# Second feed-forward block in two phases, with the down product as seven block products summed partly by adding transfers

## The chip, the cores and the metric

The kernel runs on one core of one Trainium2 chip. The metric is device time in microseconds (us). The engines are TensorE (PE, with its weight loads PEld), VectorE (DVE), ScalarE (ACT), GpSimd (POOL) and SyncE (SP). Before the change the median of three runs is 1737.13 us (1735.81 to 1737.99).

## The reference, cut to what matters

Two layers of a backbone over 512 latent and 256 context tokens, width 1024. Each layer is a mixer and then a gated feed-forward block (FFN); the change lies mainly in the FFN of the second layer, which computes only the 512 latent tokens.

```
def _swiglu(h, w_gate, w_up, w_down):
    return (jax.nn.silu(h @ w_gate) * (h @ w_up)) @ w_down
...
        x_lat = x_lat + m_lat[5] * _rms(_swiglu(h_lat, ffn_w_gate[l], ffn_w_up[l], ffn_w_down[l]), norm_post_ffn[l])
```

The hidden width is 2816, that is 22 chunks of 128 (NFC) or 11 pairs. All data are float32.

## The kernel before, in words

Every float32 operand is split into a high part H (a cast to float32r on ACT) and a low part L (a subtraction on DVE, x - H); a product is three matmuls, H by H, H by L and L by H (`mm3`). All matmuls are issued in the helper at L348, so groups of the profile go by tile names.

**The FFN** (`ffn`, called once for each layer). `first` computes the gate and up values of the first pair of chunks directly. Then, for each further pair, `product` makes the gate values (`go`) and the up values (`uo`) of 256 hidden columns for all tokens by `seven`: a block product of two by two blocks with seven instead of eight multiplications (a Strassen-Winograd form). Each of its seven blocks is 4 chunks by 3 matmuls, 12 matmuls of n = 256 columns in layer 1 and of 384 in layer 0. `seven` uses four accumulators: A and B are the two halves of one PSUM tile of two banks, `ab`; E and D are banks of their own (`sc`). A takes blocks 11, U2 and V in turn; between them ACT copies it out (L791, L801), DVE adds B to the result (L799), E (L806) and A again (L808, L809).

`pair_operands` makes what `seven` multiplies: it loads two columns of weights, each 512 KB, into two buffers `raw` (L749), adds and subtracts their halves on DVE (L752: `ws`, `raw`) and splits the sums into H (ACT, L727) and L (DVE, L728: three of 1024 columns, `wL`, and one of 512, `dL`). There are three `raw` buffers in a ring, so a load waits until the buffer of the third load before it has had its last reader; of the first weight column of a product that is the third split.

Between the gate and the up product of a pair, `acc_part` multiplies the gated values of the pair before by two row units of the down weights (128 by 1024 each, loaded and split at L671 to L673) and adds the result to `y` in SBUF: per pair 4 token tiles, 2 units, 2 column halves and 3 matmuls, 48 matmuls of 512 columns in layer 1, and a DVE addition per tile (L820). The gated values themselves are split at L1525 and L1526. After the last pair, `ending` normalises each tile of `y`, adds the residual and stores it (`post_norm`, L652 to L659).

The order on each engine is set by a list scheduler when the program is built; each engine then works strictly in that order. PSUM has eight banks: `mm` two tiles of two banks, `sc` two, `tr` two. In the second mixer, `gate` writes two token tiles into the two halves of one `mm` tile and ACT reads each half (L1418).

Of the kernel before, what the change touches and what calls it, by code (L numbers as in the profile page):

```python
# [26 lines left out]
NFC = DFF // P  # L27
EPS = 1e-6
WU = 1024
# [104 lines left out]
class Attention:  # L134
# [7 lines left out]
    half = (slice(0, 64), slice(64, P))  # L142
# [174 lines left out]
class Net:  # L317
# [3 lines left out]
    def __init__(self, ctx, tc, I, out):  # L321
        self.tc, self.nc, self.I, self.out = tc, tc.nc, I, out
        tc.nc.scalar.preload_act_table_set("silu_and_others")
        self.side = 0
        self.whole = False
        self.pinned = False
        self.turns = []
        pool = lambda name, bufs=1, **k: ctx.enter_context(tc.tile_pool(name=name, bufs=bufs, **k))
        self.cst = pool("cst")
        self.wp = pool("wp")  # L330
        self.sm = pool("sm", 4)
        self.ps = pool("ps", space=PSUM)
        self.dr = pool("dr", space=bass.MemoryType.DRAM)

    def pool(self, name, bufs=1):
        return self.tc.tile_pool(name=name, bufs=bufs, reuse_waits="tile")

    def open_pool(self, name, side="left"):
        return self.tc.alloc_tile_pool(name=name, bufs=1, side=side, reuse_waits="tile")

    def pin(self, r):

# [4 lines left out]
    def mm(self, *a, **k):  # L347
        return self.pin(self.nc.tensor.matmul(*a, **k))  # L348
# [330 lines left out]
    def mm3(self, out, stat, mov, first, last):  # L679

        mm = self.mm
        mm(out, stat[0], mov[0], start=first, stop=False)
        mm(out, stat[0], mov[1], start=False, stop=False)
        mm(out, stat[1], mov[0], start=False, stop=last)

    def gemm_T(self, pt, W, h, groups, o=0):

# [77 lines left out]
            "U2": quarter(c, 0), "S4": quarter(c, 1), "V": quarter(d, 0),  # L765
        }

    def seven(self, W, h, X, fill, then=None):

        nc, n = self.nc, h.n  # L770
        ab = self.mm_tile("ab")
        bank = {"A": ab[:, :n], "B": ab[:, 512 : 512 + n]}
        c11, c12, c21, c22 = (X[:, i, n * k : n * k + n] for i in range(2) for k in range(2))
        for wn, hn, x in SEVEN:
            new = wn in ("11", "U1", "12", "22")
            if x not in bank:
                bank[x] = self.sc_tile(x, "ED".index(x))[:, :n]
            pt = bank[x]
            (wH, wL), (hH, hL) = W[wn], h.tiles[hn]
            for k in range(4):  # L780
                for i, (a, b) in enumerate(((wH, hH), (wH, hL), (wL, hH))):
                    self.mm(
                        pt,
                        a[:, k, :],
                        b[:, k, :],
                        start=new and k == 0 and i == 0,
                        stop=k == 3 and i == 2,
                        skip_group_check=True,
                    )
            if wn == "11":  # L790
                nc.scalar.copy(c11, pt)  # L791
            elif wn == "U1":
                copy = nc.scalar.copy(c22, pt)
                if then is not None:
                    with self.tc.issue_after(copy.ins):
                        then()
                fill()
            elif wn == "12":
                nc.vector.tensor_tensor(c11, c11, pt, op=ALU.add)  # L799
            elif wn == "U2":  # L800
                nc.scalar.copy(c12, pt)  # L801
            elif wn == "22":
                nc.scalar.mul(c21, pt, -1.0)
                fill()
            elif wn == "S4":
                nc.vector.tensor_tensor(c12, c12, pt, op=ALU.add)  # L806
            else:
                nc.vector.tensor_tensor(c21, c21, pt, op=ALU.subtract)  # L808
                nc.vector.scalar_tensor_tensor(c22, pt, -1.0, c22, op0=ALU.mult, op1=ALU.subtract)  # L809
# [501 lines left out]
    def odd_mixer(self, h, fi):  # L1311
# [4 lines left out]
        with self.pool("hg") as gp:  # L1316
# [89 lines left out]
            def gate(c0, early):  # L1406
                us = self.wide_units(4 * D + c0)
                for t0 in (0, 2):
                    pt = self.mm_tile("nat").rearrange("p (a b) -> p a b", a=2)
                    s = self.wp.tile([P, WU], F32, tag="mraw", bufs=2, name="silu").rearrange("p (a n) -> p a n", a=2)  # L1410

                    def apply(x, t0=t0, s=s):
                        o = fi[:, t0 + x.start : t0 + x.stop, c0 : c0 + 512]
                        nc.vector.tensor_tensor(o, o, s[:, x, :], op=ALU.mult)

                    for a in range(2):
                        self.wide_tile(pt[:, a, :], us, h, t0 + a)
                        nc.scalar.activation(s[:, a, :], pt[:, a, :], AF.Silu)  # L1418
# [85 lines left out]
    def ffn(self, l, xp, yp, fp, pp, rp, h, ending, extra=None):  # L1504
# [7 lines left out]
        singles = [(i,) for i in range(len(tiles))]  # L1512

        gp = rp if l else fp

        def gu(x):
            return fp.tile([P, 2, 2 * n], F32, tag=x, bufs=2 if x == "go" else 1, name=x)
# [70 lines left out]
        tp.release()  # L1588
        if gp is not rp:
            rp.release()  # L1590
        end, follow, pool = ending(y)

        last = [gated(pool, k, g, u) for k in range(2)]
# [6 lines left out]
        next(follow, None)  # L1600
        if gp is rp:
            rp.release()
        return y

    def run(self):
# [11 lines left out]
        def xat(x):  # L1617
            return lambda t: x[t * P : (t + 1) * P, :]
# [132 lines left out]
        def project(l, order, yp, w, cat, xsrc):  # L1751

            rp = self.open_pool(f"r{l}")
            forms = Forms(self, order, yp.tile([P, len(order), D], F32, tag="y", bufs=1, name=f"f{l}"), rp)
            if l:
                forms.gated = [forms.gated_tiles(rp, k) for k in range(2)]
# [53 lines left out]

        def ending(ys):
            ep = self.open_pool("e1b")
            end = ender(ep, 1, 5, lat, xat(x1), lambda t: out[0, t * P : (t + 1) * P, :], None)

            def close():
                yield
                yield
                yield
                yield
                ep.release()  # L1820

            return end, close(), ep

        self.ffn(1, ha, yp, fp, pp, rp, forms, ending)
        fp.release()
        yp.release()
        ha.release()
        pad.release()


@with_exitstack
# [46 lines left out]
```

## Time and profile before

| | before |
|---|---|
| median of 3 runs | 1737.13 us |
| the profiled execution | 1736.12 us, span 1734.3 us |
| PE busy | 1682.6 us (97%), 13512 matmuls |
| DVE busy | 1287.2 us (74%) |
| ACT busy | 865.9 us (50%) |
| POOL busy | 73.6 us (4%) |
| DMA | 187.22 MB, mean 108 GB/s |

Busy shares are averages over many stages. A matmul's own duration overlaps its neighbours', so the pace of PE is read from the distance of starts, or from a chain of waits that runs through PE (x12 in 1.44 us). Granted clock of PE: 0.997.

### The profile page before, as it was taken

To read this page: it belongs to the slowest core of one execution; us is meant where nothing else is said; L and a number is where in the kernel's file an instruction comes from. 1 tells how busy PE (TensorE), PEld (TensorE's weight loads), DVE (VectorE), ACT (ScalarE), POOL (GpSimd) and SP (SyncE) were. 2 spreads that over 40 slices of the span, in tenths; PEclk is the share of its full clock that TensorE was granted. 3 is DMA by queue.
4 is the path that set the end of the run, shared out by engine and by line. 5 is a ranking of instruction groups with operands and counts; after the bars stand their busy time and mean duration, and the time that the engine had idled before them with its cause. 6 is when DMAs were issued, how large, how long until landed. Compare 5 with 4: busy or idle time off the path is not lost. (4 is left out here: it accounts for less than half of the span.)

```text
span 1734.3 us, 32373 instructions
## 1 busy us (share of the span) xinstructions
PE 1682.6 (97%) x13512; PEld 1507.3 (87%) x13512; DVE 1287.2 (74%) x2061; ACT 865.9 (50%) x1496; POOL 73.6 (4%) x93
## 2 busy tenths in 40 slices
PE   6999998999999999999999999999999999999998
PEld 5899987888999888898997888889888899999997
DVE  4889668836969999796668328887865678878785
ACT  4745568746443323233346436665644654444442
POOL 1004110000000000000001000000000000000000
PEclk9999999999999999999999999999999999999999
DMA  9641022134334455452225222111114333233333
GB/s 320 195 142 39 2 64 89 58 134 146 112 95 146 138 185 167 131 180 62 74 85 190 78 73 62 45 55 51 51 61 145 110 108 100 87 107 105 97 106 122
DMA packets 169838, 187.22 MB, mean 108 GB/s; under 512 B 6454, under 2 KB 141148, under 8 KB 169692
## 3 DMA queue, kind: packets, MB, share of 16 engines
q1 hardware_dynamic: 167760, 181.56, 33.8%
q10 hardware_dynamic: 1932, 3.59, 0.6%
q8 instruction: 106, 1.74, 0.4%
q14 instruction: 40, 0.33, 0.1%
HBM read 175.66 MB, written 9.46 MB: 107 GB/s over the span
## 5 line engine op out<-in xcount | busy, mean ns | idle before, releaser
L348 PE MATMUL nat<-wH,x 128*128 128x256 f32 (+2 forms) x944 | 216.2, 319 | 5.1 <-ACT x L641 2.6
L673 DVE TENSOR_TENSOR wL<-raw,wH 128x1024 fp32r<-128x1024 f32 (+1 forms) x126 | 150.9, 1205 | 91.8 <-ACT wH L672 91.2
L727 ACT CAST wH<-raw 128x1024 fp32r<-128x1024 f32 x120 | 124.6, 1051 | 174.9 <-PE acc L348 61.3
L728 DVE TENSOR_TENSOR wL<-raw,wH 128x1024 fp32r<-128x1024 f32 x120 | 145.0, 1220 | 63.9 <-ACT wH L727 63.9
L348 PEld LDWEIGHTS nat<-wH,x 128*128 128x128 f32 x944 | 157.6, 190 | 21.5 <-ACT x L641 3.6
L348 PE MATMUL acc<-wH,gH 128*128 128x512 f32 x440 | 172.7, 393 | 0.0
L348 PE MATMUL acc<-wH,gL 128*128 128x512 f32 x440 | 171.7, 390 | 0.0
L348 PE MATMUL acc<-wL,gH 128*128 128x512 f32 x440 | 171.6, 390 | 0.0
L672 ACT CAST wH<-raw 128x1024 fp32r<-128x1024 f32 (+1 forms) x126 | 128.9, 1039 | 82.5 <-PE nat L348 25.2
L348 PE MATMUL nat<-wL,x 128*128 128x256 f32 (+2 forms) x472 | 148.6, 315 | 0.0
L820 DVE TENSOR_TENSOR y<-y,acc 128x1024 f32<-128x1024 f32 x135 | 114.6, 861 | 28.6 <-PE acc L348 25.9
L530 DVE SCALAR_TENSOR_TENSOR macc<-mraw,scT,macc 128x1024 f32<-128x1024 f32 x98 | 123.0, 1277 | 7.3 <-DMA mraw<-in_mod_w_dram 7.1
L348 PE MATMUL ff<-x,wH 128*128 128x512 f32 (+1 forms) x512 | 127.6, 340 | 0.0
L600 POOL TENSOR_TENSOR rs<-ms,neghalf 128x1 f32<-128x1 f32 (+2 forms) x62 | 57.5, 929 | 1586.2 <-DVE ms L598 1586.0
L348 PE MATMUL oproj<-wH,x 128*128 128x512 f32 x320 | 101.5, 395 | 0.0
L348 PEld LDWEIGHTS acc<-wH,gH 128*128 128x128 f32 x440 | 82.6, 188 | 19.9 <-DVE ws L752 1.7
L348 PEld LDWEIGHTS acc<-wH,gL 128*128 128x128 f32 x440 | 82.6, 188 | 17.3
L348 PEld LDWEIGHTS acc<-wL,gH 128*128 128x128 f32 x440 | 82.7, 188 | 16.2
L348 PEld LDWEIGHTS ff<-x,wH 128*128 128x128 f32 x512 | 87.4, 190 | 10.1
L348 PEld LDWEIGHTS nat<-wL,x 128*128 128x128 f32 x472 | 89.8, 190 | 5.1
L923 ACT COPY qkh<-arr 128x512 f32<-128x512 f32 x112 | 70.1, 642 | 36.3 <-DVE arr L928 32.2
L348 PE MATMUL ff<-x,wL 128*128 128x256 f32 (+1 forms) x256 | 86.2, 337 | 0.0
(344 smaller groups left out, 4043.0 us busy)
## 6 DMA issues: line engine op xcount, KB each, us to landing
mraw<-in_mod_w_dram SPq DMA_DIRECT2D x80, 512.0 KB, 4.0
raw<-in_ffn_w_gate_dram SPq DMA_DIRECT2D x44, 512.0 KB, 3.9
raw<-in_ffn_w_up_dram SPq DMA_DIRECT2D x44, 512.0 KB, 4.4
raw<-in_ffn_w_down_dram SPq DMA_DIRECT2D x44, 512.0 KB, 3.5
raw<-in_odd_w_in_dram SPq DMA_DIRECT2D x40, 512.0 KB, 3.8
mraw<-in_mod_w_dram SPq DMA_DIRECT2D x32, 256.0 KB, 6.0
raw<-in_even_w_in_dram SPq DMA_DIRECT2D x16, 512.0 KB, 3.8
x<-xr SPq DMA_DIRECT2D x14, 512.0 KB, 2.8
```

The lines of the kernel that those rows point to most:

```text
L348: return self.pin(self.nc.tensor.matmul(*a, **k))
L530: nc.vector.scalar_tensor_tensor(a, u, w, a, op0=ALU.mult, op1=ALU.add)
L600: nc.gpsimd.tensor_tensor(rs, ms, self.neghalf.to_broadcast([P, w]), op=ALU.pow)
L672: nc.scalar.copy(H[:, :m], raw[:, :m])
L673: nc.vector.tensor_tensor(L[:, :m], raw[:, :m], H[:, :m].bitcast(F32), op=ALU.subtract)
L727: self.nc.scalar.copy(H, f)
L728: self.nc.vector.tensor_tensor(L, f, H.bitcast(F32), op=ALU.subtract)
L820: nc.vector.tensor_tensor(y, y, pt, op=ALU.add)
L923: nc.scalar.copy(qkv[:, :, :, half, :], dst)
```

## The change

1. **Phase 1 (`ffn_whole`, layer 1 only).** The same `first` and the same ten pairs by `seven`, but no `acc_part` between them. All gated values stay in SBUF as float32 (`G`, 11 pairs by 2 by 512 tokens). In the last three pairs six 256 KB pieces of the down weights are loaded ahead into `early`.
2. **Phase 2 (`down`).** The whole down product is one block product of two by two blocks with seven multiplications: tokens in two halves, hidden chunks even and odd, output columns in two halves. Each of the seven products runs over 11 chunks and 2 token tiles with 3 matmuls of 512 columns, 66 matmuls. The products, in order, are 11, N3, S1, SN, 22, S3, 12. Products 11, SN and S3 accumulate in the banks X, N3 and 22 in O, S1 and 12 in Q.
3. **The sums of weight blocks** are made by DMAs that add to SBUF (`accum_op=ALU.add`), issued by POOL: 7 in product 11 (`tb` += block 01), 14 in S1 (`tb` += block 11, and `tc` = block 01 as a plain load), 14 in SN (`tb` += block 10, `tc` += block 11). `tb` is used by S1, SN and 22, `tc` by S3. The seven transfers of a set follow the seven groups of chunks (1, 1, 2, 2, 2, 2, 1 chunks; a chunk of one block is 256 KB).
4. **The sums of gated values** and all splits are made for each product and group anew, at most three groups ahead (`ahead(3)`; `wL`/`wH` four buffers, `aL`/`aH` three).
5. **PSUM banks.** Inside both FFNs A has two banks of its own, B the one `mm` tile, and in layer 1 the up product uses the `tr` banks for E and D. In the mixer's `gate` each token tile has an `mm` tile of its own.
6. **The end.** Two token tiles are finished after S3, two in product 12; of the last tile the square sum and the gating are done by halves, the first half ahead of time.

```
 def seven(...):
-        ab = self.mm_tile("ab")
-        bank = {"A": ab[:, :n], "B": ab[:, 512 : 512 + n]}
+        bank = {"A": self.ps.tile([P, 512], F32, tag="one", bufs=2, name="a")[:, :n]}
...
-                bank[x] = self.sc_tile(x, "ED".index(x))[:, :n]
+                bank[x] = (self.mm_tile("b") if x == "B" else self.tr_tile(x) if turned else self.sc_tile(x, "ED".index(x)))[:, :n]
...
 def mm_tile(self, name):
-        return self.ps.tile([P, 1024], F32, tag="mm", bufs=2, name=name)
+        return self.ps.tile([P, 1024], F32, tag="mm", bufs=1 if self.narrow else 2, name=name)
...
 def gate(c0, early):
-                    pt = self.mm_tile("nat").rearrange("p (a b) -> p a b", a=2)
...
+                        pt = self.mm_tile("nat")[:, :512]
+                        self.wide_tile(pt, us, h, t0 + a)
+                        nc.scalar.activation(s[:, a, :], pt, AF.Silu)
...
+    def ffn_whole(self, l, xp, yp, fp, pp, rp, h, ending):
...
+        for idx in range(1, np_):
+            c0 = 2 * idx
+            g = other if idx % 2 else go()
+            self.seven(self.pair_operands(tp, wg, c0 * P, [tp], 2), h, g, nothing, todo)
...
+            x = G[:, idx]
+            self.seven(self.pair_operands(tp, wu, c0 * P, [tp], 2), h, x, nothing, None, True)
...
+    def down(self, dp, G, early, y, tiles, n, ending):
...
+        add = lambda o, src: self.pin(nc.gpsimd.dma_start(out=o, in_=src, accum_op=ALU.add))
...
+        seven = (("11", "X"), ("N3", "O"), ("S1", "Q"), ("SN", "X"), ("22", "O"), ("S3", "X"), ("12", "Q"))
...
+            nc.scalar.copy(H, src)
+            nc.scalar.copy(a[0], f)
+            v.tensor_tensor(L, src, H.bitcast(F32), op=ALU.subtract)
+            v.tensor_tensor(a[1], f, a[0].bitcast(F32), op=ALU.subtract)
+            if name == "11":
+                v.tensor_tensor(f, A[1, 0][:, i], f, op=ALU.subtract)
+                add(t[:, i], B(0, 1, i))
+            elif name == "S1":
+                add(t[:, i], B(1, 1, i))
+                self.pin(nc.gpsimd.dma_start(out=t3[:, i], in_=B(0, 1, i)))
+            elif name == "SN":
+                add(t[:, i], B(1, 0, i))
+                add(t3[:, i], B(1, 1, i))
...
+                elif name == "S3":
+                    plus(y1[:, low], b)
+                    plus(y1[:, high], b, ALU.subtract)
+                    end(y1, tiles[nh + i])
+                    if i == nh - 1:
+                        close = final(dp, y0, tiles[i])
+                else:
+                    plus(y0[:, low], b)
+                    if i < nh - 1:
+                        end(y0, tiles[i])
+                    else:
+                        close()
```

Three places in the built order carry the prediction. The first is DVE in the steady part of the pairs of layer 1. Before, while PE runs the gate product, DVE stands like this (`go` is the product being emptied, the other rows prepare the next one), and the y additions of `acc_part` follow:

```order
L799 TENSOR_TENSOR go<-go,ab 128x256
L752 TENSOR_TENSOR ws<-raw 128x512
L752 TENSOR_TENSOR raw<-raw 128x512
L728 TENSOR_TENSOR dL<-ws,dH 128x512
L752 TENSOR_TENSOR raw<-raw 128x512
L728 TENSOR_TENSOR wL<-raw,wH 128x1024
L806 TENSOR_TENSOR go<-go,E 128x256
L752 TENSOR_TENSOR raw<-raw 128x512
L728 TENSOR_TENSOR wL<-raw,wH 128x1024
L808 TENSOR_TENSOR go<-go,ab 128x256
L809 SCALAR_TENSOR_TENSOR go<-ab,go 128x256
L728 TENSOR_TENSOR wL<-raw,wH 128x1024
```

After, one product of phase 1 on DVE is the whole of the following; `b`, `E` and `a` are the banks of the product being emptied (its output here is `early`), all other rows prepare the next product.

```order
L759 TENSOR_TENSOR ws<-raw 128x512
L805 TENSOR_TENSOR early<-early,b 128x256
L759 TENSOR_TENSOR raw<-raw 128x512
L735 TENSOR_TENSOR wL<-raw,wH 128x1024
L759 TENSOR_TENSOR raw<-raw 128x512 x2
L735 TENSOR_TENSOR wL<-raw,wH 128x1024
L812 TENSOR_TENSOR early<-early,E 128x256
L735 TENSOR_TENSOR wL<-raw,wH 128x1024
L814 TENSOR_TENSOR early<-early,a 128x256
L815 SCALAR_TENSOR_TENSOR early<-a,early 128x256
L735 TENSOR_TENSOR dL<-ws,dH 128x512
```

What moved: nothing of another product stands between the first use of a pair of loads (`ws`, which needs both) and the third split, which frees the first `raw` buffer; the y additions and the splits of gated values and row units are gone from between.

The second place is POOL in phase 2, in product SN. Before, POOL has no DMA at all; after, these stand in one row (`tb` and `tc` are the sums of weight blocks):

```order
L1707 DMA tb<-in_ffn_w_down_dram 128x512
L1707 DMA tc<-in_ffn_w_down_dram 128x512
L1707 DMA tb<-in_ffn_w_down_dram 128x2x512
L1707 DMA tc<-in_ffn_w_down_dram 128x2x512
L1707 DMA tb<-in_ffn_w_down_dram 128x2x512
```

What moved: the additions that form the blocks stand on POOL and the DMA queue, and the transfers for `tb`, needed in the next product, alternate with those for `tc`, needed one product later.

The third place is DVE where product S3 ends and product 12, the last, begins. The first two rows belong to the second group of product 12; `y` takes the banks of S3 (`x_17213` and `x_17214`); `pn`, `ms` and `xr` normalise two finished tiles; the rows with `wL<-raw` and `aL` that follow are the third group of product 12.

```order
L1736 TENSOR_TENSOR wL<-raw,wH 128x512
L1737 TENSOR_TENSOR aL<-G,aH 128x256
L1761 TENSOR_TENSOR y_17205<-y_17205,x_17213 128x512 x2
L1761 TENSOR_TENSOR y_17205<-y_17205,x_17214 128x512
L659 TENSOR_TENSOR pn<-y_17205,gv_18070 128x1024
L605 TENSOR_SCALAR ms<-sq 128x1
L1761 TENSOR_TENSOR y_17205<-y_17205,x_17214 128x512
L666 SCALAR_TENSOR_TENSOR xr_18072<-pn,rs,xr_18072 128x1024
L1736 TENSOR_TENSOR wL<-raw,wH 128x1024
L659 TENSOR_TENSOR pn<-y_17205,gv_18070 128x1024
L605 TENSOR_SCALAR ms<-sq 128x1
L1737 TENSOR_TENSOR aL<-G,aH 128x512
```

What moved: normalising of two tiles, which before followed the last down product, now stands on DVE ahead of operands that the last product needs.

More of the change, by code (lines that the diff above doesn't have):

```diff
@@ L339, in open_pool, with banks @@
         return self.tc.alloc_tile_pool(name=name, bufs=1, side=side, reuse_waits="tile")
+    def banks(self, narrow):
+        if self.ps is not None:
+            self.ps.release()
+        self.narrow = narrow
+        self.ps = self.tc.alloc_tile_pool(name={True: "psn", False: "psw", None: "pso"}[narrow], bufs=1, space=PSUM, reuse_waits="tile")
     def pin(self, r):
@@ L677, in unit_cols, with mm3 @@
         return self.unit(w[:, c0 : c0 + n].rearrange("(k p) m -> p k m", p=P), KD, n, to=to)
-    def mm3(self, out, stat, mov, first, last):
+    def mm3(self, out, stat, mov, first, last, **k):
         mm = self.mm
-        mm(out, stat[0], mov[0], start=first, stop=False)
-        mm(out, stat[0], mov[1], start=False, stop=False)
-        mm(out, stat[1], mov[0], start=False, stop=last)
+        mm(out, stat[0], mov[0], start=first, stop=False, **k)
+        mm(out, stat[0], mov[1], start=False, stop=False, **k)
+        mm(out, stat[1], mov[0], start=False, stop=last, **k)
     def gemm_T(self, pt, W, h, groups, o=0):
@@ L1514, in ffn @@
         gp = rp if l else fp
+        self.banks(True)
         def gu(x):
@@ L1590, in ffn @@
             rp.release()
+        self.banks(False)
         end, follow, pool = ending(y)
```

200 lines of the change are left out of this document (183 added, 17 removed).

## Prediction

> **What bounds the kernel now.** First the head of the page, for the bound of the whole, then the second FFN, where the change lies, by its chain of waits and by stretches.
>
> ```profile
> PE 1682.6 (97%) x13512; PEld 1507.3 (87%) x13512; DVE 1287.2 (74%) x2061; ACT 865.9 (50%) x1496; POOL 73.6 (4%) x93
> ```
>
> PE is busy for 97% of the span, so matmuls that go away pay, unless something else takes their place. The chain of waits through one period of the second FFN (one pair of chunks), with columns start, duration, what:
>
> ```profile
> 1578.31 0.69 DVE y L820
> 1579.00 2.28 DVE wL L728 x2
> 1581.30 4.90 DMA raw<-in_ffn_w_up_dram
> 1586.22 1.06 ACT wH L727
> ...
> 1590.00 0.33 DVE uo L808
> ...
> 1593.00 1.20 DVE gL L1526 x2
> 1594.20 0.34 DVE go L799
> 1594.59 1.70 PE ab L348 x12
> 1596.29 0.12 PE D L348
> 1596.41 1.44 PE E L348 x12
> 1597.85 1.44 PE ab L348 x12
> 1599.29 10.92 PE acc L348 x48
> ```
>
> A block of twelve 256-column matmuls takes 1.44 us (0.120 each), 48 of 512 columns take 10.92 (0.2275 each). PE waits once per product for DVE's L799, which empties B, since A and B are one tile; and the chain runs through a weight load of 4.9 us and the splits behind it, so the ring of three `raw` buffers is already near the edge. By stretches (length, then busy PE, PEld, DVE, ACT):
>
> ```profile
> 1535.41:1567.37 31.96, 31.57 (x218) 29.29 (x217) 25.59 (x37) 14.12 (x22) 0.00 (x0) 1.00 0.34 99
> ```
>
> A period has 168 x 0.120 + 10.92 = 31.08 us of matmuls, so of 31.96 some 0.9 is waiting. Over the stage, from its first block product to its last matmul:
>
> ```profile
> 1395.02 0.40 PE L348 MATMUL ab<-b,wH 128*128 128x256 f32 x2
> ```
> ```profile
> 1704.87 20.44 PE acc L348 x90
> ```
>
> The last 96 matmuls end at 1704.87 + 96 x 0.2275 = 1726.7, so the stage takes 331.7 us. Its work is 20 products x 10.08 + 528 x 0.2275 = 201.6 + 120.1 = 321.7; **10.0 us are waits**.
>
> **The change part by part.** Sums are against the profiled execution (span 1734.3, run 1736.1); the median of the runs shown is 1.0 above it.
>
> *Matmuls.* Seven products of 66 instead of 528: 462 x 0.2275 = 105.1, **15.0 us less**. Phase 1 and 2 are then 306.7 us of PE work, without waits 25.0 less than now.
>
> *The A/B wait* of the second FFN goes with the two tiles, inside those 10.0 us; what is late next is the weight ring. Per product DVE must do, from the landing of the second load to the freeing of the first buffer (first order listing): two 512-column additions, split, two additions, split, E, split, with B between. The chain rows give 1.14 per split of 1024 (x2 in 2.28), 0.60 per 512 columns (x2 in 1.20), 0.33 per 256. So 4 x 0.60 + 2 x 0.33 + 2 x 1.14 + 1.22 = 6.56 us, and only then is the next second load issued. Its time to landing, for this stage:
>
> ```profile
> raw<-in_ffn_w_down_dram SPq DMA_DIRECT2D x20, 512.0 KB, 3.5
> raw<-in_ffn_w_up_dram SPq DMA_DIRECT2D x19, 512.0 KB, 4.8
> raw<-in_ffn_w_gate_dram SPq DMA_DIRECT2D x18, 512.0 KB, 3.9
> ```
>
> With 3.9 (the gate loads, which like these follow no other load) and 0.1 of handovers a turn is 10.56 against 10.08 of PE. Eighteen such turns lose 8.6; the second operand of a product is ready 2.9 us before PE wants it at first, and that is eaten before PE waits: **+6**. Ends: 3.5 gives 0, 4.8 gives 11.46 per turn, 24.8 - 2.9 = 22. DVE itself has room: of its 25.6 us in a period about 9 (y, row units, `gL`) leave, so some 17 stand in 20.2.
>
> *The seam of the phases.* The first `aL` stands on DVE behind the last product's L808 and L809 (0.33 each), two multiplications (0.60 each) and itself (0.33), and PE has nothing else: **+2.4**, between 1.5 and 4.
>
> *DVE at the start of the last product* (third listing). Time zero is the end of S3. y additions of bank one end at 0.6 and of bank two at 1.2, `pn` at 2.4; `ms` needs the square sum, which ACT ends at about 2.9 behind two casts, so 3.1; addition 3.7; then `xr`, behind POOL:
>
> ```profile
> 1720.18 1.28 DVE L659 SCALAR_TENSOR_TENSOR xr<-pn,rs,xr 128x1024 f32<-128x1024 f32 x1 [0.73 <-POOL rs L600]
> 1722.63 1.06 ACT L608 ACTIVATE junk<-y 128x1024 bf16<-128x1024 f32 x1 [4.55 <-DVE y L820]
> ```
>
> to 5.0; split of `wL` 6.1, `pn` 7.3, `ms` 7.4, `aL` 8.0. PE has groups one and two, 6 matmuls each, until 2.7 and waits till 8.0; the next group costs 0.4 more: **+5.7**, between 0 (the rows hide) and 7.
>
> *The adding transfers.* Before has none, so their price is open. Low end: as plain ones at the best rate seen here, the GB/s of slices of 0.9 us around the last loads:
>
> ```profile
> GB/s 0 0 37 370 431 412 412 136 0 0 0 0 0 0 0 0 19 0 0 0 0 70 412 117 0 211 356 300 337 197 346 52 370 229 0 0 323 276 0 0
> ```
>
> 512 KB at 412 GB/s are 1.27 us. High end: one after the other, each at the 3.5 us to landing of a down load. A product lasts 15.0 us. S1's first transfer can leave when its first split is done, two groups ahead, 26 us after phase 2 begins; the last sum that product 22 needs is due at about 71. In these 45 us run, in units of 512 KB, 5.5 plain loads, 5.5 additions in S1 and 10.5 in SN: 21.5 units, so **2.1 us a unit is free**. An addition reads two things, so I take twice the plain price, 2.54 (nearer to the low end, since the waits leave several in flight): 5.5 x 1.27 + 16 x 2.54 = 47.6, **+2.6**; ends 0 and 30. The 7 additions of product 11 have a whole product to land in.
>
> *Other stages.* First-layer FFN, waits for A/B, and the second mixer's gate:
>
> ```profile
> PE ab L348 <- DVE go L799: 2.5, 4, 1.0
> PE ab L348 <- DVE uo L799: 2.3, 3, 1.1
> PE ab L348 <- ACT go L791: 0.6, 1, 0.6
> PE ab L348 <- ACT go L801: 0.6, 1, 0.6
> PE ab L348 <- ACT uo L791: 0.2, 1, 0.2
> PE ab L348 <- ACT uo L801: 0.2, 1, 0.2
> ```
> ```profile
> 592.00:638.00 46.00, 44.06 (x228) 38.37 (x227) 43.76 (x55) 15.32 (x21) 0.00 (x0) 1.00 0.52 159
> ```
> ```profile
> PE nat L348 <- ACT silu L1418: 2.1, 2, 1.4
> ```
>
> In the first FFN 6.4 us are shown; but DVE is 95% busy there, and the one `mm` tile must now be emptied within the 2.73 us that the next token tile takes: I take **-2**, between +3 and -6.4. In the gate each half now has a tile: **-2.1** (0 to -2.1).
>
> *At nothing.* `early` loads hide under phase 1 (DMA share 0.34); splits of product 11 to 12 need some 13 of each 15 us on DVE (4 splits of 1024, 7 of 512, 3 of 256 make 9.8, the sums of gated values 3.4 more, two y additions 1.2) and less on ACT: without that cover each us over 15 counts once a product. From the last matmul to the end nothing is gained: half of the last normalising is ahead, but it stands behind another tile's (within 1).
>
> *Sum.* Second FFN 306.7 + 6 + 2.4 + 5.7 + 2.6 = 323.4, against 331.7: -8.3. With -2.1 and -2: -12.4, that is 1723.7 for the profiled execution and **1725 us** for the median.
>
> **A rule to weigh.** In the rows of DVE, a form with one tensor input runs faster than one with two:
>
> ```profile
> L728 DVE TENSOR_TENSOR wL<-raw,wH 128x1024 fp32r<-128x1024 f32 x120 | 145.0, 1220 | 63.9 <-ACT wH L727 63.9
> L528 DVE TENSOR_SCALAR macc<-mraw,scT 128x1024 f32<-128x1024 f32 x14 | 10.2, 746 | 0.0
> ```
>
> The Trainium skill (SBUF — State Buffer, Who interferes with whom) says that VectorE's two-port modes shut GpSimd out of a shared port, and its summary of rules advises against hiding a GpSimd-issued DMA under VectorE work. By it alone the additions would wait for gaps of DVE, as in the first rival below. The same section excepts `tensor_tensor`, for descriptor writing by inference only; DVE's long rows in phase 2 are all of that form, and at 1220 ns they agree that no fast mode is used. No run before the change shows the two side by side.
>
> **The rivals.**
> 1. *The additions come late (slower).* Place: `tb` for product 22, behind 28 transfers on one queue. If each takes 3.5 us, serial or held up by DVE, 21.5 x 3.5 = 75 instead of 45: 30 late instead of 2.6, **1752 us**. It eats the whole gain from (45 + 2.6 + 12.4) / 21.5 = 2.8 us a unit. For it: no addition has been timed, and DVE is nearly full. Against: 412 GB/s seen, several transfers in flight.
> 2. *The ring holds up phase 1 more*: loads at 4.8 us, 22 instead of 6, **1741**. For: the up loads in this stage; against: they overlapped a down load, which is gone.
> 3. *No new wait*: ring 0, additions 0: **1716**. For: DVE has idle time in phase 1; against: the ring sum above.
> 4. *It doesn't do what it says*: excluded for the matmuls, whose rows in the built order number 462; the wait for B could return on another bank, which is within the range of the first FFN.
>
> **How the numbers follow.** Forecast 1725 (1718 to 1733): 0.52. Rival 3: 0.18. Rival 2: 0.08. Rival 1 in any size: 0.22. The range, 1713 to 1755, takes in rival 3 and rival 1 at its price and leaves out what is faster (ring, additions, seams all at their low ends with 6 us from the first FFN) and a queue worse than 3.5 us: about 0.2. A difference under 0.2% (3.5 us) cannot be told from none. Faster: nearly all of the forecast and rival 3, 0.66; same: the edges of the forecast and some of rivals 1 and 2, 0.09; slower: 0.25.
>
> **What would show it.** Phase 1: 20 products in 201.6 to 208; a `ws` that waits about 1 us for its load each product shows the ring, and PE waits for `wL` from there. Seam: PE idle some 2.4 before the first X matmul. Phase 2: products of 15.0, product 12 of 20.7 with one gap of about 5 behind `aL`. Additions: time to landing of the POOL DMAs, and DVE or ACT waiting for `tb` in product 22; a gap there above 3 us is rival 1. Gate and first FFN: the waits quoted gone. Wrong would be above all a `tb` wait in every group, or a first FFN that grew.

## The result: slower by 0.57%

Beside each other on one chip, the changed kernel takes 1744.91 us (median of 4 runs, 1742.7 to 1745.75) and the kernel before 1736.47 us (4 runs, 1732.15 to 1737.99): ratio **1.0057, interval 1.0043 to 1.0071**. The prediction was 1725 us, and faster. The profiled execution of the changed kernel took 1742.7 us with a span of 1740.9, that is 6.6 us more than the span before. Ratios leave out one execution of a later kernel, e10, that took 3307.84 us.

From the page of the changed kernel: the busy times, PE and the DMA engines in 40 slices of the span, and POOL's DMA queue.

```profile
PE 1675.3 (96%) x13446; PEld 1500.4 (86%) x13446; DVE 1298.3 (75%) x2103; ACT 896.4 (51%) x1552; POOL 108.6 (6%) x128
...
PE   6999999999999999999999999999999999999887
...
DMA  9641022134334455452235121211224253334993
...
q0 software_dynamic: 6896, 14.42, 4.1%
```

The 66 matmuls that were to go are gone. But PE falls to eight and seven tenths in the last three slices; in the first two of these the DMA engines, at three to five tenths through the second FFN until then, stand at nine.

Phase 1 of the changed kernel, 161.28 us out of its middle (length, then busy PE, PEld, DVE, ACT, POOL, granted clock, DMA share, GB/s), has no gap at all: 16 products of 10.08 us.

```profile
1434.57:1595.85 161.28, 161.28 (x1347) 161.28 (x1346) 135.20 (x210) 87.74 (x143) 0.00 (x0) 1.00 0.34 100
```

Phase 2 by its seven products, in their order 11, N3, S1, SN, 22, S3, 12 (same columns; each stretch runs from a product's first matmul to the next one's, the last to 0.8 us behind the last matmul):

```profile
1597.23:1616.41 19.18, 16.74 (x68) 13.43 (x67) 15.39 (x28) 6.39 (x11) 7.12 (x7) 0.91 1.04 302
1616.41:1640.24 23.83, 18.13 (x67) 13.17 (x66) 13.57 (x20) 11.88 (x20) 2.65 (x5) 0.93 0.83 230
1640.24:1655.20 14.96, 14.96 (x67) 12.39 (x66) 10.48 (x14) 9.79 (x18) 8.13 (x10) 1.00 1.05 234
1655.20:1670.21 15.01, 15.01 (x68) 12.31 (x66) 11.92 (x18) 8.75 (x15) 9.03 (x10) 1.00 1.10 246
1670.21:1694.22 24.01, 18.39 (x67) 12.06 (x66) 11.13 (x16) 9.21 (x15) 7.81 (x7) 1.00 0.99 180
1694.22:1711.89 17.67, 15.88 (x68) 12.15 (x66) 14.52 (x23) 10.45 (x18) 0.00 (x0) 1.00 0.16 47
1711.89:1733.90 22.01, 17.16 (x67) 13.18 (x65) 18.36 (x24) 9.98 (x17) 1.98 (x3) 0.92 0.42 142
```

A product's work is 15.0 us. S1 and SN take just that; product 11 takes 4.2 more, **N3 8.8**, **22 9.0**, S3 2.7 and 12 6.2 (to its last matmul, 1733.1). That is 30.9 us of delay in 105 us of work. What PE waited for in phase 2:

```profile
PE o L355 <- ACT aH L1735: 9.6, 7, 3.7
PE x L355 <- DVE aL L1737: 4.1, 3, 2.4
PE q L355 <- DVE wL L1736: 2.9, 1, 2.9
PE q L355 <- DVE aL L1737: 1.3, 1, 1.3
PE o L355 <- DVE wL L1736: 1.2, 5, 0.2
```

These idle times come to 19.1 us. They are counted from the modelled end of the matmul before, 0.39 us or more behind its start, while the pace is 0.2275; so a part of each wait does not show. PE's rows behind one gap in product 22 (start, duration), and DVE's there:

```profile
1677.32 0.39 PE L355 MATMUL o<-wH,aL 128*128 128x512 f32 x1
1678.94 0.50 PE L355 MATMUL o<-wH,aH 128*128 128x512 f32 x1 [1.23 <-ACT aH L1735]
1679.68 0.50 PE L355 MATMUL o<-wL,aH 128*128 128x512 f32 x1 [0.24 <-DVE wL L1736]
1680.28 0.50 PE L355 MATMUL o<-wH,aL 128*128 128x512 f32 x1
1680.62 0.40 PE L355 MATMUL o<-wH,aH 128*128 128x512 f32 x1
```
```profile
1678.40 1.23 DVE L1736 TENSOR_TENSOR wL<-tb,wH 128x1024 fp32r<-128x1024 f32 x1 [3.31 <-ACT wH L1734]
1679.54 0.68 DVE L1737 TENSOR_TENSOR aL<-G,aH 128x512 fp32r<-128x512 f32 x1
```

The starts behind the gap are 0.74, 0.60 and 0.34 us apart. The first two are waits as well: `wL` ends at 1679.63 and the matmul that reads it starts at 1679.68; `aL` ends at 1680.22 and its matmul starts at 1680.28. So the place costs about 2.4 us, nearly all of it waiting for ACT and DVE behind one late sum. Counted by the distance of starts in this way, some 25 of the 30.9 us are waits for casts and splits. Another 4.5 us come from the clock: in products 11, N3 and 12 there is a stretch of 3.41 us each with a granted clock of 0.50, in which the starts lie 0.43 us apart. This is the one in product 11:

```profile
1599.90:1603.31 3.41, 2.90 (x7) 2.33 (x8) 3.41 (x9) 1.22 (x2) 1.97 (x2) 0.50 1.00 369
```

The last us or so is not explained.

**N3** waits for its own plain loads. The chain of waits there, and the DMA engines from 1594 to 1640 us in 40 slices:

```profile
1604.94 7.72 DMA raw<-in_ffn_w_down_dram
...
1614.11 13.93 DMA raw<-in_ffn_w_down_dram
```
```profile
DMA  0038989999999999999999999999999833241549
GB/s 0 0 87 258 290 294 385 411 406 387 280 255 255 269 258 278 306 289 258 256 267 262 272 292 301 262 256 265 264 260 392 342 123 125 69 173 30 198 150 315
```

Before, a load of 512 KB took 3.5 us to land; here one of 256 KB takes 7.7 from issue to landing and one of 512 KB 13.9. The engines are full from 1598 to 1629; while plain loads are alone they move about 400 GB/s, and as soon as the additions of product 11 join in, 260.

**Product 22** waits for the sums in `tb`. From 1668 to 1692 nothing but additions runs (first line); the second is from a kernel below, in which the same transfers are plain (1645 to 1662):

```profile
DMA packets 2504, 4.78 MB, mean 199 GB/s; under 512 B 172, under 2 KB 172, under 8 KB 2504
```
```profile
DMA packets 1816, 6.46 MB, mean 380 GB/s; under 512 B 242, under 2 KB 242, under 8 KB 1815
```

In both, the engines are full. An addition of 512 KB takes 524 288 B at 199 GB/s = 2.63 us, a plain transfer 1.38.

**Product 12** waits behind the post-normalising on DVE. The chain of waits there:

```profile
1715.42 1.28 DVE xr L666
...
1716.70 0.36 DVE wL L1736
...
1717.75 1.22 DVE pn L659
...
1719.03 0.61 DVE aL L1737
...
1719.69 10.16 PE q L355 x37
```

### The profile page after: what moved, and what is told of

It reads as the page before. It is cut to its first block, busy times and chain, and to the rows that moved or that the text cites. A ratio compares the mean times of both kernels' runs of the same rounds, so it can differ in the third digit from the quotient of the medians.

```text
span 1740.9 us, 32512 instructions
## 1 busy us (share of the span) xinstructions
PE 1675.3 (96%) x13446; PEld 1500.4 (86%) x13446; DVE 1298.3 (75%) x2103; ACT 896.4 (51%) x1552; POOL 108.6 (6%) x128
## 4 chain that ended last, share of the span: by engine, by line
PE 77%; DVE 9%; DMA 6%; ACT 4%; issue 2%; POOL 1%; SPq 0%; POOLq 0%; DVEq 0%; ACTq 0%
PE nat L355 12%; PE a L355 10%; PE acc L355 8%; PE ff L355 8%; PE E L355 7%; PE oproj L355 5%; PE D L355 3%; PE b L355 3%; PE fq L355 2%; PE gqk L355 2%; PE S L355 1%; PE pearly L355 1%; DMA tb<-in_ffn_w_down_dram 1%; DMA raw<-in_ffn_w_down_dram 1%; PE poh L355 1%
## 5 line engine op out<-in xcount | busy, mean ns | idle before, releaser
L680 DVE TENSOR_TENSOR wL<-raw,wH 128x1024 fp32r<-128x1024 f32 (+1 forms) x104 | 124.3, 1203 | 82.5 <-ACT wH L679 81.6
L679 ACT CAST wH<-raw 128x1024 fp32r<-128x1024 f32 (+1 forms) x104 | 106.8, 1038 | 81.1 <-PE nat L355 23.7
L355 PE MATMUL acc<-wH,gH 128*128 128x512 f32 x264 | 104.6, 397 | 1.3 <-DVE y L826 0.8
L355 PE MATMUL acc<-wL,gH 128*128 128x512 f32 x264 | 103.2, 391 | 1.4 <-DVE wL L680 1.4
L355 PE MATMUL acc<-wH,gL 128*128 128x512 f32 x264 | 103.2, 391 | 0.0
L355 PEld LDWEIGHTS ff<-x,wH 128*128 128x128 f32 x512 | 87.4, 190 | 10.1
L826 DVE TENSOR_TENSOR y<-y,acc 128x512 f32<-128x512 f32 (+1 forms) x81 | 68.9, 861 | 22.4 <-PE acc L355 21.1
L759 DVE TENSOR_TENSOR raw<-raw 128x512 f32<-128x512 f32 x120 | 82.5, 688 | 2.0
L934 DVE TENSOR_TENSOR arr<-arr,f 128x512 f32<-128x512 f32 x112 | 74.2, 686 | 1.9 <-ACT qkh L929 0.3
L355 PE MATMUL a<-T,wH 128*128 128x384 f32 (+1 forms) x320 | 70.3, 309 | 0.7 <-ACT G L797 0.7
```

The costliest lines, as they stand in the source:

```text
L679: nc.scalar.copy(H[:, :m], raw[:, :m])
L680: nc.vector.tensor_tensor(L[:, :m], raw[:, :m], H[:, :m].bitcast(F32), op=ALU.subtract)
L759: add = lambda o, x, y: nc.vector.tensor_tensor(o, x, y, op=ALU.add)
L826: nc.vector.tensor_tensor(y, y, pt, op=ALU.add)
L934: nc.vector.tensor_tensor(dst, dst, tb, op=ALU.mult)
```

## The experiments

Ratios are to the kernel before on the same chip; the changed kernel has 1.0057, and 0.001 is 1.7 us. From one profile to the next phase 2 begins up to 7 us earlier or later (1593.0 to 1599.9 where phase 1 is unchanged), so the lengths of single products are compared in the traces, and whole kernels by their ratios.

### Without the sums, and with plain transfers in their place

```
-        add = lambda o, src: self.pin(nc.gpsimd.dma_start(out=o, in_=src, accum_op=ALU.add))
+        add = lambda o, src: None                                              # e1
+        add = lambda o, src: self.pin(nc.gpsimd.dma_start(out=o, in_=src))     # e2
```

> The changed kernel with every adding transfer left out (tb and tc keep their first blocks, so the down product is not the reference's); all plain loads stay. The throughput theory (an addition costs the DMA engines twice a plain transfer of its size, and they are full from the first microsecond of phase 2): product 22 runs in 15 us instead of 24.0, S3 in 15 to 16 instead of 17.7, N3 in 15 to 18 instead of 23.8; the kernel ends 17 to 21 us earlier, at 1722 to 1726. The rival that the plain loads alone swamp the start of phase 2 (5.5 units of 512 KB for tb, 5.5 for N3, xr and gv): N3 stays near 23, only 22 and S3 recover, about 1731. If neither holds, 1743 as the changed kernel.

> The changed kernel with each addition turned into a plain transfer of the same bytes from the same queue (tb and tc are overwritten, not added to, so the down product is not the reference's). The throughput theory: the same 16 units cost 1.3 us each instead of 2.55, so product 22 runs in 15 to 16 us and N3 in 16 to 20: 1724 to 1730. The rival that POOL's transfers are late because POOL issues them while DVE is nearly full: kind of transfer is all the same, 22 and N3 stay at 24, 1742 to 1745.

e1: 1722.77 us, **0.9935** (0.9912 to 0.9958). e2: 1724.56 us, **0.9943** (0.9922 to 0.9964). N3 and 22 of e1, then of e2:

```profile
1613.13:1631.13 18.00, 16.42 (x66) 12.27 (x67) 15.46 (x24) 12.22 (x22) 0.00 (x0) 1.00 0.65 225
1661.09:1676.05 14.96, 14.96 (x68) 12.39 (x66) 14.33 (x22) 8.88 (x15) 0.00 (x0) 1.00 0.00 0
```
```profile
1615.32:1633.88 18.56, 16.13 (x67) 12.16 (x66) 13.51 (x20) 11.88 (x20) 2.15 (x4) 1.00 0.67 231
1663.88:1678.84 14.96, 14.96 (x68) 12.39 (x66) 14.33 (x22) 8.88 (x15) 0.00 (x0) 1.00 0.09 34
```

The additions cost about 21 us, and it is that they **add** which costs: the same bytes from the same queue beside the same DVE work, without the addition, cost 1.4, which lies within the intervals. So neither the queue nor DVE's work holds them up. In e2's SN, where DVE is busy for 12.2 of 15.0 us, POOL's plain transfers move 378 GB/s. The Trainium skill (SBUF — State Buffer, Who interferes with whom) has VectorE's two-port modes shut GpSimd out but excepts `tensor_tensor`; that exception fits what was seen here. Of N3's 8.8 us about 3 stay with no addition at all, though the plain loads then move near 400 GB/s. Of the 5.8 us that go, about 1.6 are the stretch at half clock, which e1 doesn't have in N3.

### The order of the sums

e7 moves the additions to `tc` from SN to product 22; e6 moves the additions of product 11 to N3.

```
             elif name == "SN":
                 add(t[:, i], B(1, 0, i))
+            elif name == "22":                   # e7
                 add(t3[:, i], B(1, 1, i))
```
```
                 v.tensor_tensor(f, A[1, 0][:, i], f, op=ALU.subtract)
+            elif name == "N3":                   # e6
                 add(t[:, i], B(0, 1, i))
```

> The changed kernel with the tc additions issued in product 22 in place of SN, so that the tb additions, which are needed a product earlier, don't share the queue and the engines with them. Throughput theory: 5.5 units of 2.55 us have 15 us and a product's lead, so product 22 runs in 15 to 16 us and S3 in 15 to 17: 8 to 12 us less than the changed kernel, ratio 0.998 to 1.001. Rival (the sums are late since they start late, whatever their order): 22 keeps over 20 us, ratio over 1.003.

> The changed kernel with the seven additions of product 11 issued one product later, in N3. Throughput theory: during product 11 the DMA engines then carry plain loads alone, N3's raw blocks come about 14 us earlier, and N3 shrinks from 23.8 to 16 to 19 us; product 22 stays at 24 (its sums leave one after the other at 2.55 as before): 5 to 8 us less than the changed kernel, ratio 1.001 to 1.003. Rival (the plain loads alone are the burst): N3 stays above 22, and S1 may wait for its sums, ratio 1.005 or more.

e7: 1730.32 us, **0.9984** (0.9975 to 0.9993). e6: 1741.61 us, 1.0050 (1.0032 to 1.0067). Products 22 and S3 of e7, then N3 of e6:

```profile
1668.01:1682.97 14.96, 14.96 (x67) 12.39 (x66) 12.98 (x19) 9.91 (x16) 8.38 (x9) 1.00 1.13 206
1682.97:1698.21 15.24, 15.24 (x67) 12.31 (x66) 12.21 (x19) 9.84 (x17) 1.21 (x2) 1.00 0.65 132
```
```profile
1619.29:1642.78 23.49, 18.52 (x68) 13.20 (x66) 13.57 (x20) 11.81 (x20) 2.38 (x5) 0.93 0.83 230
```

e7 settles product 22. All additions are still there and still 206 GB/s, but the ones that are needed first are no longer mixed one to one with those that are needed a product later: 9.0 us in product 22 and 2.4 in S3 are gone. e6 misses, and its trace shows that the additions leave no later than before: the first of the seven additions leaves 3.9 us behind the first matmul of phase 2 and the last two from 17.8 us on, in the changed kernel 3.8 and 17.6. So whether later additions would spare N3 is not tested by it.

### Less traffic at the start of phase 2

Groups five to seven of product 11 are loaded twice, into `tb` and into `raw`. e9 reads `tb`.

```
-                if i.stop <= 6:
-                    src = early[:, i]
-            if name in ("N3", "12") or name == "11" and i.stop > 6:
+                src = early[:, i] if i.stop <= 6 else t[:, i]
+            if name in ("N3", "12"):
```

> The changed kernel in which groups five to seven of product 11 read tb in place of a second copy of the same blocks in raw (2.5 units of 512 KB fewer at the start of phase 2, and the raw buffers are free for N3 from the beginning). Theory (N3 starves because tb's plain loads, its own raw loads and the additions of product 11 share engines that move 260 GB/s while additions run): 3.2 us less of traffic and three blocks of N3 ahead of the additions, N3 from 23.8 to 17 to 20 us, ratio 1.002 to 1.004. Rival (the wait is only the ring of three raw buffers, whatever the engines carry): N3 at 15 to 16, ratio 0.9995 to 1.001; or the additions take whatever is free, N3 above 22 and ratio over 1.0045.

1737.86 us, **1.0022** (1.0013 to 1.0031). N3:

```profile
1613.87:1633.14 19.27, 16.66 (x68) 12.24 (x66) 12.18 (x18) 9.76 (x17) 2.21 (x5) 1.00 0.83 223
```

N3 loses 4.6 us, as the theory of full engines has it: by the distance of starts 3.0 of waits and 1.6 of the stretch at half clock, which is not there in this trace. It is not the ring of `raw` buffers alone, since then N3 would have come to 15 or 16.

### The normalising behind the splits of product 12

```
                 ahead(3)
+                if p == 6 and at in (4, 8):
+                    i3 = at // 4 - 1
+                    end(y[:, nh + i3, :], tiles[nh + i3])
+                    if i3 == nh - 1:
+                        close = final(dp, y[:, i3, :], tiles[i3])
...
-                    end(y1, tiles[nh + i])
-                    if i == nh - 1:
-                        close = final(dp, y0, tiles[i])
```

> The changed kernel with the two post-normalisings of S3's tiles moved behind the operand splits of product 12 (the first behind those of its fifth group, the second behind the last). Theory: product 12 loses the waits for wL and aL (2.9 + 1.3 us) and the slow matmuls behind them (2.8): from 22.0 to 15 to 17.5 us, the kernel 4 to 7 us earlier, 1736 to 1739. Rival (DVE has no room in this product at all, so the wait only moves to its end or into the last normalising): within 1.5 us of 1743.

1739.69 us, **1.0029** (1.0018 to 1.0039). Product 12, and from its last matmul to the end:

```profile
1711.01:1728.20 17.19, 15.95 (x67) 12.06 (x65) 16.60 (x23) 10.00 (x17) 1.96 (x2) 1.00 0.36 128
1728.20:1737.90 9.70, 0.04 (x1) 0.00 (x0) 4.43 (x8) 0.72 (x2) 1.10 (x2) 0.68 0.54 204
```

Product 12 goes from 21.2 to 17.2 us; the end, 7.8 in the changed kernel, becomes 9.7. These two stretches give 2.1 us; the ratios differ by 4.9, and where the rest lies is open. There the chain of waits goes through the store of the second normalised tile and the load of the next one into one of the two `xr` buffers:

```profile
1727.08 2.77 DMA out_dram<-xr
...
1729.87 3.16 DMA xr<-x
```

### The accumulator banks

e4 is the kernel before with only the bank changes (A, B and the gate). e5 is the changed kernel with A and B of its second FFN in one tile again.

```
-        ab = self.mm_tile("ab")                                                     # e4: taken out, as in the change
-        bank = {"A": ab[:, :n], "B": ab[:, 512 : 512 + n]}
+        bank = {"A": self.ps.tile([P, 512], F32, tag="one", bufs=2, name="a")[:, :n]}
```
```
-        self.banks(True)                                                            # e5, in ffn_whole
+        self.banks(False)
...
+            ab = self.mm_tile("ab")
+            bank = {"A": ab[:, :n], "B": ab[:, 512 : 512 + n]}
```

> The kernel before with only the accumulator banks changed as in the changed kernel (A and B apart, each gate half a tile of its own, narrow banks during the FFNs); the down product stays as it was. Theory: the second FFN's waits for ab (most of its 10.0 us) go, the gate gains 2.6 and the first FFN 1.2, its opening loses 3 as in the changed kernel: 1724 to 1728. Rival (the weight ring takes the place of the wait, since here a down load stands between the others): second FFN gains 3 or less, 1732 to 1735.

> The changed kernel with A and B of the second FFN in one tile again (the rest, the down product by itself above all, stays). Theory after the last runs (the waits for ab were DVE's arrears in a stage that also split down rows and added y, so they go with the down rows, not with the banks): phase 1 stays at 20 products of 10.08 to 10.2 us, the kernel within 3 us of the changed one, ratio 1.004 to 1.007. Rival (the prediction's: one tile makes each product wait for DVE's L799 whatever else DVE has to do): some 0.5 us for each of 20 products, 10 us more, ratio 1.010 to 1.013.

e4: 1734.71 us, **1.0002** (0.9989 to 1.0014). e5: 1753.83 us, **1.0116** (1.0101 to 1.0132). What PE waited for in e4's second FFN, and then one row of e5's phase 1 and its waits:

```profile
PE acc L355 <- DVE y L826: 4.3, 7, 1.1
PE acc L355 <- DVE go L812: 0.8, 2, 0.6
```
```profile
1434.57:1595.85 161.28, 156.48 (x1274) 153.58 (x1272) 133.58 (x204) 84.84 (x135) 0.00 (x0) 1.00 0.34 97
```
```profile
PE ab L355 <- DVE G L809: 4.0, 6, 1.9
```

In the second FFN the separate banks alone are worth nothing: the waits for `ab` go and waits for `acc` come, since the `mm` tile that is left must now be emptied by DVE's `y` addition; the last matmul of that FFN ends 322.2 us behind the first one of its first down unit, 321.4 before. In the whole of e4 what they give in the first FFN behind its opening (5.3 us) and in the mixer with the gate (2.2) is lost in the openings of the two FFNs (4.3 and 2.8; see below). Without the separate banks the changed kernel would be 10 us slower still: a product takes 10.6 us in the mean, in place of 10.1, and its X product starts 211.7 us behind the first block product instead of 202.7. So in this FFN the banks' gain exists only together with the down rows' leaving. The theory that I had written against the prediction's own for e5 fell.

### The opening of the FFNs

In the changed kernel PE's opening of the second FFN is 3.0 us longer (31.5 us from its first matmul to the first block product, 28.6 before). From its first matmul to the last transposes, before and after:

```profile
1366.46:1376.25 9.79, 7.74 (x66) 7.55 (x64) 7.61 (x11) 7.14 (x15) 1.10 (x2) 1.00 0.89 267
```
```profile
1363.00:1372.32 9.32, 5.33 (x45) 5.15 (x44) 7.00 (x10) 5.83 (x13) 1.10 (x2) 0.94 0.89 274
```

21 matmul records have moved from ahead of the transposes to behind them, so PE waits 4.0 us for `xn` in place of 2.1. In the first FFN the same happens: its opening takes 41.0 us, 36.9 before, with a wait for `xn` of 4.0 in place of 1.6. Both openings of the changed kernel also have matmuls at a granted clock of 0.50, for 3.4 us in the first and 6.8 in the second; before it was none and 3.4. e8 opens the narrow banks behind the opening, which puts them back:

```
         tp = first()
+        self.banks(True)
```

> The changed kernel with the switch to narrow banks behind the opening products of both FFNs in place of ahead of them, so that the 21 matmuls which had moved behind the last transposes stand ahead of them again. Theory: PE's waits of 4.0 us for xn go back to 1.6 and 2.1, and the slow matmuls behind them go: first FFN's opening 5 us shorter, second's 3: ratio 0.9995 to 1.002. Rival (the order is the same in effect and the matmuls only change places): within 2 us of the changed kernel, ratio over 1.0045.

1741.97 us, 1.0048 (1.0031 to 1.0065): the interval holds no change as well as 4 us. The trace shows the wait for `xn` at 2.1 us again, and another that took its place, since the banks are now switched where PE has nothing else:

```profile
PE a L355 <- DVE G L1642: 2.4, 1, 2.4
PE hT L358 <- DVE xn L624: 2.1, 1, 2.1
```

### Together

e10 takes the edits of e7, e3 and e9. e11 is another order, 11, N3, 12, S1, SN, 22, S3, with the edits of e6, e7 and e9; in it the first two token tiles are normalised in product 22, and no half of the last normalising is ahead. e12 is e10 with all loads of the down product, and the two of `xr`, in the order of the program.

```
+        seven = (("11", "X"), ("N3", "O"), ("12", "Q"), ("S1", "O"), ("SN", "X"), ("22", "Q"), ("S3", "X"))   # e11
```
```
-        nc.sync.dma_start(out=xt, in_=xsrc(t))                                     # e12
+        self.pin(nc.sync.dma_start(out=xt, in_=xsrc(t)))
...
-        load = lambda o, src: nc.sync.dma_start(out=o, in_=src)
+        load = lambda o, src: self.pin(nc.sync.dma_start(out=o, in_=src))
```

> The changed kernel with three mends at once: tc additions in product 22, post-normalising of S3's tiles behind the splits of product 12, no second copy for product 11. Theory (the three waits are apart from each other, so what each gave alone adds up): 9 + 5 + 4 to 7 us less than the changed kernel, 1721 to 1727, ratio 0.993 to 0.9965. Rival (one wait covers another): a gain of under 12 us, ratio above 0.9985.

> Product 12, which needs no sum, in third place (11, N3, 12, S1, SN, 22, S3); additions of product 11 issued in N3, those of tc in 22, no second copy; y0 tiles are normalised during product 22, and the last normalising has no half ahead. Throughput theory: by the start of S1 the engines have 45 us for 16.5 plain units and 5.5 additions (35 us) where the changed kernel had 30 us for 35 us of them, and no later product needs more than 14 of its 15 us: N3 at 16 to 20 us, every other product at 15 to 16, tail 1 to 2 us longer: ratio 0.989 to 0.993 (1718 to 1724). Rival (additions stretch whatever runs beside them, product by product): N3 or 12 above 20 us, ratio over 0.996.

> The three mends of the last runs, and the two 512 KB loads of xr, which stood at the start of phase 2 though nothing needs them before product 12, sent in program order (so all loads of the down product are, N3's first two no longer ahead of tb's). Theory (N3 waits because the engines are full, so 2 units of 512 KB fewer in the queue at that time bring its blocks some 2.5 us earlier): N3 from 20.1 to 16.5 to 18.5 us, ratio 0.991 to 0.993. Rival (what N3 waits for is its place behind tb in the queue, and it has that place now): N3 at 20 to 23, ratio 0.993 to 0.996.

e10: **1721.84 us, 0.9933** (0.9914 to 0.9951), faster than both kernels; the three waits are indeed apart from each other. e11: 1725.23 us, 0.9958 (0.9945 to 0.9971). e12: 1732.70 us, 0.9990 (0.9978 to 1.0002). N3 in e10, in e11 and in e12, and the wait that cost e12 its gain:

```profile
1611.27:1631.39 20.12, 17.84 (x67) 13.10 (x66) 12.27 (x18) 9.77 (x17) 3.32 (x5) 0.92 0.88 223
```
```profile
1614.83:1634.93 20.10, 17.41 (x67) 13.43 (x66) 12.85 (x19) 9.00 (x15) 0.85 (x1) 0.92 0.85 227
```
```profile
1617.09:1636.33 19.24, 16.92 (x68) 12.07 (x67) 12.58 (x19) 10.86 (x18) 1.79 (x5) 1.00 0.84 226
```
```profile
PE q L355 <- ACT wH L1733: 6.4, 1, 6.4
```

In e11 product 12 takes 15.6 us, but N3 keeps its delay: as in e6, the additions of product 11 leave no later than before (3.4 to 18 us behind the start of phase 2). And the end behind the last matmul grows from 7.8 to 9.5 us. In e12, 1 MB less of traffic brings N3 0.9 us and not 2.5, and that is the granted clock (1.00 against 0.92): by the distance of starts the waits in N3 are 3.6 us, in e10 3.4. The expected cause is not seen, though the order of N3's first loads changed with it. The kernel loses far more in product 12, where the load of a `raw` block now stands on SP behind a store that waits for the normalising on DVE. What is left of N3's delay, 4 to 5 us, is not settled between plain traffic and the additions beside it; a version in which the additions of product 11 begin only when N3's last block has landed was not tried.

## Why the prediction was wrong, point by point

The terms in us, forecast against the two profiled executions:

| term | forecast | measured |
|---|---|---|
| matmuls that go | -15.0 | -15.0 |
| waits of before in the second FFN | -10.0 | -10.0 |
| weight ring in phase 1 | +6 | +1.1 (ten pairs in 202.7 instead of 201.6) |
| seam, start of product 11 | +2.4 | +4.2 |
| N3 | 0 | +8.8 |
| sums: product 22, and S3 behind it | +2.6 | +11.7 |
| DVE queue in product 12 | +5.7 | +6.2 |
| gate | -2.1 | -2.3 |
| ahead of the first FFN | 0 | +1.1 |
| opening of the first FFN | 0 | +4.1 |
| first FFN behind its opening | -2 | -6.5 |
| opening of the second FFN | 0 | +3.0 |
| from the last matmul to the end | 0 | +0.2 |

The measured terms add up to +6.6, and so much do the spans differ. The +1.1 ahead of the first FFN belongs to no part of the change that is known; it can be the difference of two executions.

- **Matmuls and waits of before: right.** They go, and PE has no gap in the 16 products shown of phase 1. The reason given for the second, "goes with the two tiles", was half of it: e4 shows that the tiles alone give nothing there, e5 that the change needs them.
- **Ring: wrong, in the safe direction.** `ws` does wait for its loads, as the prediction's sign of the ring has it, 12.1 us in all over the 16 products shown, but PE does not. The sum let the load that completes a pair leave only behind the third split of `wL`. In the trace it leaves behind the second: that split ends at 1505.96, the load goes at 1505.99, and the next `ws`, which waits for it, starts at 1510.07; behind the third split (1507.43) goes the first load of the pair after that. (So the first buffer comes free with the second split, not with the third as the description of the kernel has it.) From 1480 to 1530 a turn is 5.4 to 6.0 us on DVE and 3.9 to 4.9 for the load, 10.0 in the mean in place of 10.56, and just fits.
- **The price of an addition: right.** Twice the plain price, 2.54 us, was taken as a choice between two ends; 2.63 was measured with additions alone, against 1.38 for plain ones.
- **The step that failed** is what was made of that price, in two places. The first is "The 7 additions of product 11 have a whole product to land in": that looks at the additions' own deadline alone. In product 11 the plain loads (5.5 units for `tb`, 2.5 of second copies, 5.5 for N3) fill 13.5 x 1.27 = 17 us by themselves, three more units go to `xr` and `gv`, and the additions came on top; N3, which uses no sum at all, paid for them (18.0 us without additions, 23.8 with). N3 was put at nothing and cost 8.8. The second is the sum of 47.6 us for 21.5 units against 45. From the first transfer of S1 (1638.18) to the last sum for product 22 (1691.20) they took 53.0, so by the prediction's own sum 8 us too long and not 2.6; product 22 lost 9.0. And the sum took the order of the queue as given: in SN the `tc` additions, not needed before S3, took every other place, so product 22 got its sums one per 5.13 us, where it uses one in 2.73 (it takes 14.96 us when they follow later, e7). The first rival had the place right, `tb` for product 22, but not the price: it wanted 2.8 us a unit or more before the gain was eaten, and at 2.6 it already was, since other terms failed beside it.
- **DVE queue in product 12: right in place; the size is in part luck.** The waits for `wL` and `aL` are 4.6 us by the distance of starts, less than the 5.7; the stretch at half clock behind them adds 1.5 and brings the term to 6.2. e3 gives back 4.0 of it, of which 2 go into the end.
- **Seam: right for the wait**, 2.44 us shown against 2.4; the other 1.5 us of product 11 are again half clock.
- **First FFN: the waits go, and more than was taken for them.** Behind its opening it is 6.5 us shorter, against 6.4 of waits shown before; its opening takes 4.1 of that back.
- **Openings: not in the sum.** Switching to the narrow banks ahead of the opening moves 21 matmuls behind a wait. The openings are 3.0 us longer in the second FFN and 4.1 in the first; e8, which puts the matmuls back, gains no more than its interval can tell from nothing.
- **A lower clock was in no term.** Of the 30.9 us of delay in phase 2 it makes 4.5, about 1.5 in each of products 11, N3 and 12.

## What to carry to other kernels

Count a DMA that adds at twice the bytes, and lay the traffic out product by product against the engines' rate, with everything that shares them in that time: the one that is late need not be the one that was added. In one queue, put transfers in the order of their deadlines; that alone (e7) was worth more than half of what the sums cost. And take the length of the matmul engine's waits from the distance of its starts and from the ends of what it reads, not from the idle time shown: here 25 us against 19.

## What the runs showed of the hardware

- Adding transfers of 512 KB run at 199 to 206 GB/s with all engines full, plain ones of the same shape from the same queue at 380. Mixed with plain loads the whole moves about 260. The 512 KB loads into `raw` at the start of phase 2 took 12.3 us in the median from issue to landing, and 4.8 in e1, without additions; but one load took 10.5 there too.
- The granted clock in these traces is 1.00 or 0.50, and it falls behind short waits, for 3.41 us in each of the three places in phase 2 of the changed kernel. It fell there at the end of a wait shown as 2.44 us in product 11 and of one of 3.7 in N3; in e1 the same 2.45 us in product 11 left it at 1.00. In product 22 of the changed kernel waits of up to 1.23 us left it at 1.00, but in the same product of e9, with waits of up to 1.2 us, two such stretches bring it to 0.86. The Trainium skill (TensorE: Matmul & The Clock Gate, Why this matters for your kernels) asks for no idle gap above about 3 us: here shorter ones lowered it in some executions and not in others.
